# A two-layer decoder trunk on one core: eight heads' values in one wide projection, 64-row score matmuls for both heads of a pair, TensorE's attention order written out

## The chip, the core and the metric

The kernel runs on one core of a Trainium2 chip. A core has five engines with instruction streams of their own: TensorE (PE, matmuls; its weight loads are listed as PEld), VectorE (DVE), ScalarE (ACT), GpSimd (POOL) and SyncE (SP, which here issues the transfers). They meet through semaphores. Operands lie in SBUF, 128 partitions wide; matmul results go to PSUM, which has 8 banks of 128 x 512 fp32. The metric is the device time of one execution in microseconds, lower is better; three runs gave 951.81 to 952.43, median 952.17.

## The reference, cut to what matters

512 tokens of 1024 channels pass two layers, the first with a pooling mixer, the second with stick-breaking attention over 16 heads of 64, each followed by a squared-ReLU MLP of width 4096. Keys and values are projected once, from the stream behind the first MLP. The attention layer is where the change lies:

```python
kv = jnp.matmul(rms_norm(x, kv_norm_g), w_kv).reshape(B, S, 2, N_HEADS, HEAD_DIM)
...
q = jnp.matmul(h, w_q[j])
...
z = jnp.einsum('bhqd,bhkd->bhqk', q_blk, k_blk) * inv_sqrt_d        # 128 queries at a time
mask = s_idx < t_idx
log1m = jnp.where(mask, -jax.nn.softplus(z), 0.0)
excl = lax.cumsum(log1m, axis=3, reverse=True) - log1m
a = jnp.where(mask, jnp.exp(jax.nn.log_sigmoid(z) + excl), 0.0)
outs.append(jnp.einsum('bhqk,bhkd->bhqd', a, v_blk))
...
m = jnp.matmul(o, w_o[j])
```

## The kernel before

**Precision.** Every large product is made from operands split into a high part, rounded to the matmul format `F32R`, and the low remainder: high x high, high x low and low x high, three matmuls, added up in PSUM (`mm3`, lines 299 to 302; `up_block`, lines 703 to 717). ACT writes the high part (a copy), DVE the low one (a subtraction). The normed stream stands transposed in `xnh` and `xnl`: 128 channels on the partitions, 8 such chunks (`KC`), 512 tokens.

**Weights.** `want` (line 187) queues the blocks, 128 x 1024 each, in the order of use; `fill` (line 246) starts fetching the next while fewer than four (`ahead`) are held. There are three buffers with the tag `w` and one with `wx`, each for a high and a low part. Most blocks of the attention stage were scaled and split during the first MLP and put to DRAM (`kept`), so they come back as two transfers of 512 KB on SP's queue, and the transfer waits until the last matmul that read the buffer is done.

**The attention stage** goes by pairs of heads, 8 of them, in an order written as a list of steps (`ATT_ORDER`, line 59):

- `V`: values. One `V` group holds 4 heads, 256 columns, and two weight blocks (`values`, line 882). The digits behind the group are the tiles of 128 tokens; `V001` is group 0, tiles 0 and 1. Each tile takes 24 matmuls of 256 columns. ACT and DVE then write the two parts to a tile of tag `v`, of which there are two.
- `N2`, `N3`: the transposes of the normed token tiles 2 and 3, which the first MLP leaves undone.
- `K0`: the first half of the key projection of pair 0, for tokens 0 to 255 (`start`, line 904).
- `P`: keys, then queries of a pair (`queries_keys`, line 931), 24 matmuls of 512 columns each. For head a, ACT writes the high part of the keys twice, to both 64-partition halves of `k`, and DVE the low part to one half of `kl`, whose other half holds zeros. The queries' high part goes to one half of `q`, their low part to the other.
- `S`: scores, weights and scan (`weights`, line 1065). With the layout of `P`, one matmul over 128 rows gives high x high and low x high at once, and one against `kl` gives high x low. Per head these are 2 matmuls for each of 4 query tiles, of 512, 384, 256 and 256 columns, in three PSUM banks (`Head.scores`, line 985). Then ACT takes two sigmoids of them (`against`, `for_`), DVE scans (line 1016) and multiplies (line 1022).
- `T`: 20 transposes of a pair's weights by TensorE into six PSUM banks (line 1035), which ACT and DVE split into `ah` and `al` (lines 1041 and 1045).
- `A`: products with the values, 16 matmuls (line 1052).
- `O`: the output projection of two pairs; the digits are token tiles. `O00123` is that of pairs 0 and 1. `E1` is the end.

On TensorE the order is kept as written only up to `P0`; behind it, the scheduler that builds the program places TensorE's instructions itself by a model of their times, as it does for the other engines. So the order in the trace differs a little from the list: scores of pair 4 stand among products of pair 3, for instance. Within the end (`END_ORDER`, line 72, from the scores of the last pair on) all engines are ordered by hand; there `z01` is the scores of head 0, bank 1.

Of the kernel before, what the change touches and what calls it, by code (L numbers as in the profile page):

```python
# [15 lines left out]
P = 128  # L16
# [89 lines left out]
def trunk(ctx, tc, x, consts, grow, pw, wup, wdn, wq, wk, wv, wo, out):  # L106
# [12 lines left out]
    def name(s):  # L119
        uid[0] += 1  # L120
        return f"{s}{uid[0]}"
# [65 lines left out]
    def want(key, src, scaled=None):  # L187
        queue.append((key, src, scaled))
# [64 lines left out]
    def get(key):  # L253
        while key not in made:
            make()
        return made.pop(key)

    for l in range(2):
        if l == 1:
            n = len(queue)  # L260
            for what, i, part in ATT_ORDER:
                if what == "V" and 0 in part:
                    for h in range(2):
                        want(("v", i, h), wv[i, h], gains(C_KV * KC + 4 * h, 4))
                elif what == "P":
                    want(("k", i), wk[i], gains(C_KV * KC, KC))
                    want(("q", i), wq[i], gains(C_MIX_PRE1 * KC, KC))
                elif what == "O" or what == "E":
# [610 lines left out]
    with tc.tile_pool(name="att", bufs=1, reuse_waits="tile") as ap:  # L879
        att_pool[0] = ap  # L880

        def values(u, part):
            if u not in vs:
                w = [get(("v", u, h)) for h in range(2)]
                vs[u] = w, ap.tile([P, T, 4, 2, HD], F32R, tag="v", bufs=2, name=name("v"))
            w, v = vs[u]
            for s in part:
                need(s)
# [7 lines left out]
                pv4 = pv[:, :256].rearrange("p (h d) -> p h d", h=4)  # L896
                nc.scalar.copy(v[:, s, :, 0, :], pv4)
                nc.vector.tensor_tensor(
                    out=v[:, s, :, 1, :], in0=pv4, in1=v[:, s, :, 0, :].bitcast(F32), op=ALU.subtract
                )  # L900

        started = {}

        def start(key):

            need(0, 1)
            started[key] = ps(), get(key)
            up_block(*started[key], slice(0, S // 2))

        def project(key):  # L910
            need(*range(T))
            if key in started:
                pq, w = started.pop(key)
                up_block(pq, w, slice(S // 2, S))
            else:
                pq = ps()
                up_block(pq, get(key), slice(0, S))
            return pq

        def qk_tile(tag):  # L920
# [2 lines left out]
        half = [slice(0, HD), slice(HD, P)]  # L923


        kls = [qk_tile(f"kl{a}") for a in range(2)]
        with tc.issue_after(latest["pool"].ins):
            for a in range(2):
                nc.gpsimd.memset(kls[a][half[1 - a], :].bitcast(F32), 0.0)

        def queries_keys(p):
            qs, ks = [], []
            pk = project(("k", p))
            for a in range(2):
                k, kl, own, other = qk_tile(f"k{a}"), kls[a], half[a], half[1 - a]
                nc.scalar.copy(k[own, :], pk[own, :])
                latest["act"] = nc.scalar.copy(k[other, :], pk[own, :])
                latest["dve"] = nc.vector.tensor_tensor(
                    out=kl[own, :], in0=pk[own, :], in1=k[own, :].bitcast(F32), op=ALU.subtract
                )  # L940
                ks.append(k)
            fill()
            pq = project(("q", p))
            for a in range(2):
                q, own, other = qk_tile(f"q{a}"), half[a], half[1 - a]
                latest["act"] = nc.scalar.copy(q[own, :], pq[own, :])
                latest["dve"] = nc.vector.tensor_tensor(
                    out=q[other, :], in0=pq[own, :], in1=q[own, :].bitcast(F32), op=ALU.subtract
                )
                qs.append(q)  # L950
            fill()
            return qs, ks
# [19 lines left out]
        class Head:  # L972
# [12 lines left out]
            def scores(self, b):  # L985
                q, k, kl = self.qk[0][self.a], self.qk[1][self.a], kls[self.a]
                pz = self.pz[b] = ps()
                o = 0
                for i in self.SCORES[b][0]:
                    n = max(256, (i + 1) * P)  # L990
                    nc.tensor.matmul(pz[:, o : o + n], q[:, TS[i]], k[:, :n], start=True, stop=False)  # L991
                    nc.tensor.matmul(pz[:, o : o + n], q[:, TS[i]], kl[:, :n], start=False, stop=True)  # L992
                    o += n

            def against(self, b):
                tiles, at = self.SCORES[b]
# [64 lines left out]
            def out(self, o):  # L1061
                own = half[self.a]
                nc.vector.tensor_tensor(out=o[own, :], in0=self.po[half[0], :], in1=o[own, :], op=ALU.add)

        def weights(p):
# [43 lines left out]
        def end():  # L1109
# [82 lines left out]
            def half_up(j):  # L1192
# [2 lines left out]

            last_heads = heads[last]
            steps = {
                "z": lambda a, b: last_heads[a].scores(b), "x": lambda a, b: last_heads[a].against(b),
                "y": lambda a, b: last_heads[a].for_(b), "sc": lambda a: last_heads[a].scan(),
                "mu": lambda a: last_heads[a].weigh(), "T": lambda a, b: last_heads[a].turn(b),  # L1200
                "ah": lambda a, b: last_heads[a].high(b), "al": lambda a, b: last_heads[a].low(b),
# [25 lines left out]

        def step(what, i, part):
            nonlocal gpost1
            if what == "V":  # L1230
                values(i, part)
            elif what == "N":
                need(i)
            elif what == "K":
                start(("k", i))
            elif what == "P":
                qk[i] = queries_keys(i)
                if i == PAIRS - 1:
                    until(("o", 5))
            elif what == "S":  # L1240
                gate[0] = True
                heads[i] = weights(i)
                fill()
            elif what == "T":
                transposed(heads[i])
                behind.update(latest)
            elif what == "A":
                mix_pair(i, vs[i // 2][1])
            elif what == "O" and part:
                out_proj(i, part)  # L1250
                if i == 0:
# [68 lines left out]
```

## Time and profile before

| | us |
|---|---|
| time, median of 3 runs | 952.17 |
| lowest and highest of them | 951.81, 952.43 |
| the profiled execution, its own time | 952.24 |
| its span, first to last instruction | 950.5 |

The page's groups of the operations that the change touches (line, engine, operation, out<-in and shape, count | busy us in total, mean ns of one | idle us before them):

```profile
L300 PE MATMUL ps<-w,xnh 128*128 128x256 f32 x128 | 36.6, 286 | 0.0
L991 PE MATMUL ps<-k,q 128*128 128x256 f32 x32 | 8.4, 284 | 0.0
L991 PE MATMUL ps<-k,q 128*128 128x512 f32 x16 | 6.5, 409 | 0.0
L938 DVE TENSOR_TENSOR kl<-ps,k 64x512 fp32r<-64x512 f32 x16 | 11.0, 685 | 15.1 <-ACT k L937 15.0
L947 DVE TENSOR_TENSOR q<-ps,q 64x512 fp32r<-64x512 f32 x16 | 11.0, 688 | 7.5 <-ACT q L946 7.2
L1016 DVE TENSOR_TENSOR_SCAN e<-u,begin 128x1280 f32<-128x1280 f32 x16 | 45.2, 2823 | 11.0 <-ACT u L1000 10.4
```

Times are microseconds from the start of the span. A matmul record lasts longer than its share of TensorE, since the next one starts before it ends; what a matmul costs in a stream is read from start to start. The attention stage runs from about 368 to 570 us, the last pair's end to about 640, between the two MLPs.

### The profile page before, as it was taken

The numbers are of one execution on the slowest core, as the hardware profiler recorded it, in microseconds if no ns is written. First come the engines' busy times: TensorE is split into PE (matmuls) and PEld (weight loads), VectorE is DVE, ScalarE is ACT, GpSimd is POOL, SyncE is SP. The second block draws the span as 40 slices with busy tenths as digits, with TensorE's granted clock in tenths as the row PEclk, the third lists the DMA queues.
The fourth block names the chain that finished last, engine by engine and source line by source line (L and its number), as shares of the span: only waits on it lengthen the run. The fifth ranks groups of instructions, "written<-read, shape, count | busy, mean of one in ns | idle before, by whom it ended". The sixth has DMA issues, their size and how long they took to land.

```text
span 950.5 us, 12510 instructions
## 1 busy us (share of the span) xinstructions
PE 940.9 (99%) x4758; PEld 799.7 (84%) x4758; DVE 707.9 (74%) x813; ACT 577.8 (61%) x1015; POOL 42.1 (4%) x85
## 2 busy tenths in 40 slices
PE   9999999999999999999999999999999999999996
PEld 7998888888888889899899988898888888888885
DVE  5875798988979976476577778874696966958756
ACT  6667979788775547456656554865545444444532
POOL 2300000000000004000000000200000000000002
PEclk9999999999999999999999999999999999999999
DMA  8244969789697760522424271442513233133102
GB/s 309 96 178 148 342 219 347 295 283 356 217 323 269 271 207 2 202 85 90 172 95 178 91 264 45 134 155 71 196 43 131 93 133 111 45 133 111 35 11 89
DMA packets 43262, 156.15 MB, mean 164 GB/s; under 512 B 4289, under 2 KB 4673, under 8 KB 43202
## 3 DMA queue, kind: packets, MB, share of 16 engines
q1 hardware_dynamic: 43202, 155.36, 46.1%
q8 instruction: 37, 0.61, 0.3%
q14 instruction: 23, 0.19, 0.1%
HBM read 121.79 MB, written 33.55 MB: 163 GB/s over the span
## 4 chain that ended last, share of the span: by engine, by line
PE 94%; DVE 2%; ACT 2%; POOL 1%; issue 1%; POOLq 0%; DVEq 0%; ACTq 0%
PE ps L589 28%; PE ps L708 15%; PE ps L712 15%; PE ps L711 15%; PE ps L300 4%; PE ps L301 4%; PE ps L302 4%; PE ps L1052 2%; PE ps L829 1%; PE ps L1035 1%; PE ps L991 1%; PE ps L395 1%; PE ps L992 1%; ACT xn L285 1%; PE ps L801 1%
## 5 line engine op out<-in xcount | busy, mean ns | idle before, releaser
L589 PE MATMUL ps<-w,a 128*128 128x512 f32 x1176 | 278.6, 389 | 0.0
L711 PE MATMUL ps<-xnh,w 128*128 128x512 f32 (+1 forms) x712 | 261.1, 369 | 0.0
L712 PE MATMUL ps<-xnl,w 128*128 128x512 f32 (+1 forms) x712 | 261.1, 368 | 0.0
L708 PE MATMUL ps<-xnh,w 128*128 128x512 f32 (+1 forms) x712 | 260.3, 368 | 0.1
L589 PEld LDWEIGHTS ps<-w,a 128*128 128x128 f32 x1176 | 220.7, 188 | 45.9 <-DVE w L282 0.2
L712 PEld LDWEIGHTS ps<-xnl,w 128*128 128x128 f32 x712 | 134.2, 189 | 21.8
L708 PEld LDWEIGHTS ps<-xnh,w 128*128 128x128 f32 x712 | 133.7, 189 | 22.4 <-DVE w L850 0.3
L711 PEld LDWEIGHTS ps<-xnh,w 128*128 128x128 f32 x712 | 133.8, 189 | 22.1
L598 DVE TENSOR_TENSOR y<-ps,y 128x512 f32<-128x512 f32 x124 | 84.5, 688 | 43.9 <-PE ps L589 43.7
L172 DVE TENSOR_TENSOR w<-raw,w 128x1024 fp32r<-128x1024 f32 x58 | 70.9, 1223 | 57.4 <-ACT w L170 57.2
L170 ACT CAST w<-raw 128x1024 fp32r<-128x1024 f32 x58 | 61.0, 1051 | 79.3 <-PE ps L708 79.2
L281 ACT CAST a<-r 128x768 fp32r<-128x768 f32 (+1 forms) x60 | 47.7, 794 | 72.1 <-PE ps L589 55.7
L282 DVE TENSOR_TENSOR a<-r,a 128x768 fp32r<-128x768 f32 (+1 forms) x60 | 54.1, 902 | 12.3 <-ACT a L281 12.1
L281 ACT CAST w<-e 128x1536 fp32r<-128x1536 f32 (+1 forms) x30 | 41.8, 1394 | 23.8 <-DVE e L563 14.4
L1016 DVE TENSOR_TENSOR_SCAN e<-u,begin 128x1280 f32<-128x1280 f32 x16 | 45.2, 2823 | 11.0 <-ACT u L1000 10.4
L282 DVE TENSOR_TENSOR w<-e,w 128x1536 fp32r<-128x1536 f32 (+1 forms) x30 | 49.5, 1649 | 1.8 <-ACT w L281 1.6
L181 ACT ACTIVATE apart<-apart,eye 128x128 f32<-128x128 f32 (+1 forms) x132 | 43.1, 407 | 0.5 <-DMA apart<-in_wk 0.5
L282 DVE TENSOR_TENSOR w<-w,w 128x1536 fp32r<-128x1536 f32 (+1 forms) x20 | 33.0, 1650 | 8.6 <-ACT w L281 8.6
L621 ACT ACTIVATE r<-ps 128x512 f32<-128x512 f32 x56 | 33.1, 591 | 8.6 <-PE ps L708 8.5
L282 DVE TENSOR_TENSOR w<-xn,w 128x1536 fp32r<-128x1536 f32 (+1 forms) x20 | 33.0, 1650 | 5.6 <-ACT w L281 5.5
L300 PE MATMUL ps<-w,xnh 128*128 128x256 f32 x128 | 36.6, 286 | 0.0
L622 ACT ACTIVATE r<-r 128x512 f32<-128x512 f32 x56 | 35.5, 634 | 1.3
(134 smaller groups left out, 1393.6 us busy)
## 6 DMA issues: line engine op xcount, KB each, us to landing
raw<-in_wup SPq DMA_DIRECT2D x64, 512.0 KB, 4.1
w<-kept SPq DMA_DIRECT2D x60, 512.0 KB, 4.2
kept<-wx SPq DMA_DIRECT2D x30, 512.0 KB, 5.0
w<-in_wdn SPq DMA_DIRECT2D x8, 1536.0 KB, 6.7
kept<-apart SPq DMA_DIRECT2D x24, 512.0 KB, 5.7
xn<-in_wdn SPq DMA_DIRECT2D x8, 1536.0 KB, 7.7
apart<-in_wk SPq DMA_DIRECT2D x7, 512.0 KB, 7.1
apart<-in_wq SPq DMA_DIRECT2D x7, 512.0 KB, 9.4
```

The costliest lines, as they stand in the source:

```text
L170: nc.scalar.copy(hi, raw)
L172: nc.vector.tensor_tensor(out=lo, in0=raw, in1=hi.bitcast(F32), op=ALU.subtract)
L181: nc.scalar.mul(c, c, gc[:, lo + k : lo + k + 1])
L281: latest["act"] = nc.scalar.copy(hi, src)
L282: latest["dve"] = nc.vector.tensor_tensor(out=lo, in0=src, in1=hi.bitcast(F32), op=ALU.subtract)
L300: nc.tensor.matmul(dst, ah, bh, start=start, stop=False)
L589: nc.tensor.matmul(bank, a[:, x, q, TS[t]], w[:, z, q], start=start and q == 0 and k == 0, stop=q == self.n - 1 and k == 2, skip_group_che ...
L598: nc.vector.tensor_tensor(out=part, in0=bank, in1=part, op=ALU.add)
L708: nc.tensor.matmul(pu[:, cols], wl[:, k, :], xnh[:, k, cols], start=False, stop=k == KC - 1)
L711: nc.tensor.matmul(pu[:, cols], wh[:, k, :], xnh[:, k, cols], start=k == 0, stop=False)
L712: nc.tensor.matmul(pu[:, cols], wh[:, k, :], xnl[:, k, cols], start=False, stop=False)
L1016: nc.vector.tensor_tensor_scan(out=self.e[:, ::-1], data0=self.u[:, 1:][:, ::-1], data1=begin[:, ::-1], initial=0.0, op0=ALU.mult, op1=ALU ...
```

## The change

1. The values of the first 8 heads are projected together, 512 columns at a time, as step `H`: `H0` adds up chunks 0 to 3, `H1` chunks 4 to 7, the digits behind are token tiles. A tile is 12 matmuls of 512 columns per step. The four weight blocks of this half are laid out anew on the host, two chunks of 512 columns in each, and are all held until the half is done; `H` ends with a `fill` of four blocks. It stands ahead of the first projections and scores. Steps `K0` and its `start` go. The other 8 heads keep `V`.
2. `queries_keys` writes high and low parts of both heads as whole 128-partition tiles (`kh`, `kl`, `qh`, `ql`): one copy on ACT and one subtraction on DVE for the keys, and as many for the queries. `scores` makes three 64-row matmuls per head and query tile, the two heads in turn, each on its own half of the partitions and into its own bank, with 512, 384, 256 and 128 columns. All scores of a pair are made before any sigmoid is issued; the order of sigmoids, scans and multiplications is altered with that.
3. TensorE's order is kept as written for the whole list, which itself is altered: `S` follows `P0` at once, `S` and `A` follow `T` at `T0`, `T1` and `T3`, and `O0` is split around `T2`. In the end the scores of both heads are one step (`z1` for `z01` and `z11`).

```diff
-    for w in """V001 N2 K0 N3 V02 P0 V03 S0 P1 T0 V101 S1 A0 P2 T1 V123 A1 S2 P3 T2 O00123 A2 S3 P4 V201 T3 A3
-    S4 P5 T4 V223 S5 A4 P6 V301 T5 S6 A5 V323 P7 T6 E1""".split()
+    for w in """H001 N2 H101 N3 H023 H123 P0 S0 P1 T0 S1 A0 P2 T1 S2 A1 P3 O001 T2 O023 S3 A2 P4 V201 T3 S4
+    A3 P5 V22 T4 V23 S5 A4 P6 V30 T5 V31 S6 A5 V323 P7 T6 E1""".split()
...
-    for w in """D6 R0 R1 z01 z00 x01 z02 x00 z11 x02 z12 y02 sc0 A60 y01 y00 x11 z10 oc60 A61 y11 x10 od60 E01 y10
+    for w in """D6 R0 R1 z1 z0 x01 z2 x00 x02 y02 sc0 A60 y01 y00 x11 oc60 A61 y11 x10 od60 E01 y10
...
+                if what == "H" and not i and 0 in part:
+                    for h in range(4):
+                        want(("v", 0, h), wv[h], gains(C_KV * KC + 2 * h, 2))
...
+        def half_values(i, part):
+            if not half_w:
+                half_w.extend(get(("v", 0, h)) for h in range(4))
+                for u in range(2):
+                    vs[u] = None, value_tile(u)
+            for s in part:
+                if i == 0:
+                    half_bank[s] = ps()
+                for k in range(4 * i, 4 * i + 4):
+                    (wh, wl), c = half_w[k // 2], NS[k % 2]
+                    mm3(
+                        half_bank[s], xnh[:, k, TS[s]], xnl[:, k, TS[s]], wh[:, c], wl[:, c], k == 0, k == KC - 1
+                    )
+                if i == 1:
+                    for u in range(2):
+                        value_parts(vs[u][1], s, half_bank[s][:, u * 256 : u * 256 + 256])
+            if i == 1 and T - 1 in part:
+                fill(ahead)
...
         def queries_keys(p):
+            both = []
+            for what in "kq":
+                src = project((what, p))
+                hi, lo = qk_tile(f"{what}h"), qk_tile(f"{what}l")
+                latest["act"] = nc.scalar.copy(hi, src)
+                latest["dve"] = nc.vector.tensor_tensor(out=lo, in0=src, in1=hi.bitcast(F32), op=ALU.subtract)
+                both.append((hi, lo))
+                fill()
+            return both
...
+        def scores(hs, b):
+            (kh, kl), (qh, ql) = hs[0].qk
+            for x in hs:
+                x.pz[b] = ps()
+            o = 0
+            for i in Head.SCORES[b][0]:
+                n = SEG[i][1]
+                for m, (x, y) in enumerate(((qh, kh), (qh, kl), (ql, kh))):
+                    for h in hs:
+                        own = half[h.a]
+                        nc.tensor.matmul(
+                            h.pz[b][:, o : o + n], x[own, TS[i]], y[own, :n], start=m == 0, stop=m == 2,
+                        )
+                o += n
...
         def weights(p):
             hs = [Head(qk[p], p, a) for a in range(2)]
+            for b in range(3):
+                scores(hs, b)
             for x in hs:
                 for b in range(3):
-                    x.scores(b)
                     x.against(b)
+            hs[0].scan()
+            for x in hs:
+                for b in range(3):
                     x.for_(b)
-                x.scan()
-                x.weigh()
+            hs[0].weigh()
+            hs[1].scan()
+            hs[1].weigh()
             return hs
...
-        first = [what for what, _, _ in ATT_ORDER].index("P") + 1
         with tc.manual_schedule(engines={mybir.EngineType.PE}):
-            for x in ATT_ORDER[:first]:
+            for x in ATT_ORDER[:-1]:
                 step(*x)
-        for x in ATT_ORDER[first:-1]:
-            step(*x)
         end()
```

More of the change, by code (lines that the diff above doesn't have):

```diff
@@ L261, in trunk @@
             for what, i, part in ATT_ORDER:
-                if what == "V" and 0 in part:
+                if what == "H" and not i and 0 in part:
+                    for h in range(4):
+                        want(("v", 0, h), wv[h], gains(C_KV * KC + 2 * h, 2))
+                elif what == "V" and 0 in part:
                     for h in range(2):
-                        want(("v", i, h), wv[i, h], gains(C_KV * KC + 4 * h, 4))
+                        want(("v", i, h), wv[2 * i + h], gains(C_KV * KC + 4 * h, 4))
                 elif what == "P":
@@ L267, in trunk @@
                     want(("q", i), wq[i], gains(C_MIX_PRE1 * KC, KC))
-                elif what == "O" or what == "E":
+                elif what == "O" and 0 in part or what == "E":
                     for c in range(2 * i, 2 * i + 2 if what == "O" else PAIRS):
@@ L880, in trunk, with value_tile, value_parts @@
         att_pool[0] = ap
+        def value_tile(u):
+            return ap.tile([P, T, 4, 2, HD], F32R, tag="v", bufs=2, name=name("v"))
+        def value_parts(v, s, src):
+            pv4 = src.rearrange("p (h d) -> p h d", h=4)
+            nc.scalar.copy(v[:, s, :, 0, :], pv4)
+            nc.vector.tensor_tensor(
+                out=v[:, s, :, 1, :], in0=pv4, in1=v[:, s, :, 0, :].bitcast(F32), op=ALU.subtract
+            )
+        half_w, half_bank = [], {}
+        def half_values(i, part):
[16 more added lines that the diff above has]
+                fill(ahead)
         def values(u, part):
             if u not in vs:
-                w = [get(("v", u, h)) for h in range(2)]
-                vs[u] = w, ap.tile([P, T, 4, 2, HD], F32R, tag="v", bufs=2, name=name("v"))
+                vs[u] = [get(("v", u, h)) for h in range(2)], value_tile(u)
             w, v = vs[u]
             for s in part:
-                need(s)
                 pv = ps()
@@ L895, in values @@
                     )
[L896 to L908, printed above, removed]
-        def project(key):
[L911 to L917, printed above, removed]
+                value_parts(v, s, pv[:, :256])
+        def project(key):
+            pq = ps()
+            up_block(pq, get(key), slice(0, S))
             return pq
@@ L923, in trunk @@
         half = [slice(0, HD), slice(HD, P)]
[L926 to L929, printed above, removed]
         def queries_keys(p):
[L932 to L952, printed above, removed]
+            both = []
[7 more added lines that the diff above has]
+            return both
         begin = ap.tile([P, NSEG], mybir.dt.bfloat16, tag="begin", name="begin")
@@ L983, in __init__ @@
                 self.pz, self.pt, self.parts, self.to = {}, {}, {}, {}
[L985 to L993, printed above, removed]
             def against(self, b):
@@ L1197, in end @@
             steps = {
-                "z": lambda a, b: last_heads[a].scores(b), "x": lambda a, b: last_heads[a].against(b),
+                "z": lambda b: scores(last_heads, b), "x": lambda a, b: last_heads[a].against(b),
                 "y": lambda a, b: last_heads[a].for_(b), "sc": lambda a: last_heads[a].scan(),
@@ L1229, in step @@
             nonlocal gpost1
-            if what == "V":
+            if what == "H":
+                half_values(i, part)
+            elif what == "V":
                 values(i, part)
@@ L1233, in step @@
                 need(i)
-            elif what == "K":
-                start(("k", i))
             elif what == "P":
@@ L1250, in step @@
                 out_proj(i, part)
-                if i == 0:
+                if gpost1 is None:
                     with tc.issue_after(latest["sp"].ins):
                         gpost1 = gain_row(R_MIX_POST1)
-        first = [what for what, _, _ in ATT_ORDER].index("P") + 1
         with tc.manual_schedule(engines={mybir.EngineType.PE}):
-            for x in ATT_ORDER[:first]:
+            for x in ATT_ORDER[:-1]:
                 step(*x)
-        for x in ATT_ORDER[first:-1]:
-            step(*x)
         end()
@@ L1289 @@
     blocks = lambda w, n: w.reshape(KC, P, -1, n).transpose(2, 1, 0, 3)
-    wv = blocks(a["w_kv"][:, D:], 256).reshape(4, P, 2, D).transpose(0, 2, 1, 3)
+    wv = np.concatenate([
+        blocks(w, n).reshape(-1, P, c, D).transpose(0, 2, 1, 3).reshape(4, P, D)
+        for w, n, c in ((a["w_kv"][:, D : D + 512], 512, 4), (a["w_kv"][:, D + 512 :], 256, 2))
+    ])
     arrays = {
```

1 line of the change is left out of this document (added).

## Prediction

> **What bounds the kernel now.** I read the page first: how busy each engine is, the granted clock, and the chain that ended last by engine.
>
> ```profile
> span 950.5 us, 12510 instructions
> PE 940.9 (99%) x4758; PEld 799.7 (84%) x4758; DVE 707.9 (74%) x813; ACT 577.8 (61%) x1015; POOL 42.1 (4%) x85
> PEclk9999999999999999999999999999999999999999
> PE 94%; DVE 2%; ACT 2%; POOL 1%; issue 1%; POOLq 0%; DVEq 0%; ACTq 0%
> ```
>
> TensorE is busy 99% of the span at full clock and holds 94% of the chain. DVE and ACT have room. So an edit pays if it shortens TensorE's own stream, and costs if it opens a hole in it. The second view is busy time by window, cut at the steps of the attention stage (a count includes a record or two that reach in from a neighbour):
>
> ```profile
> core 0: us, PE busy (x) PEld busy (x) DVE busy (x) ACT busy (x) POOL busy (x), PEclk, DMA share, GB/s
> 392.91:395.47 2.56, 2.56 (x18) 2.38 (x17) 0.42 (x1) 2.27 (x6) 0.00 (x0) 1.00 0.90 266
> 395.47:406.37 10.90, 10.90 (x50) 8.97 (x49) 9.23 (x5) 5.33 (x14) 0.00 (x0) 1.00 0.71 269
> 406.37:408.47 2.10, 2.10 (x21) 2.10 (x20) 1.65 (x3) 2.08 (x5) 0.00 (x0) 1.00 0.43 92
> 414.30:416.87 2.57, 2.57 (x19) 2.39 (x18) 0.42 (x1) 2.21 (x6) 0.00 (x0) 1.00 0.00 0
> 416.87:419.38 2.51, 2.51 (x19) 2.33 (x17) 2.02 (x1) 2.51 (x9) 0.00 (x0) 1.00 0.00 0
> 456.41:468.00 11.59, 11.55 (x51) 8.98 (x49) 4.82 (x9) 6.72 (x14) 0.00 (x0) 1.00 0.19 73
> ```
>
> In order: the 16 score matmuls of pair 0; the 48 projection matmuls of pair 1; the 20 transposes of pair 0; the scores of pair 1; the products of pair 0; the first output projection. In all but the last TensorE has no hole. The waits of the stage hold little that can be won back:
>
> ```profile
> PEld ps L300 <- DVE al L1045: 0.5, 1, 0.5
> PE ps L991 <- DVE q L947: 0.4, 1, 0.4
> ```
>
> **Part 1: the value projection.** A 24-matmul block of 256 columns against projections of 512 columns:
>
> ```profile
> 368.46:371.34 2.88, 2.88 (x26) 1.00 0.00 0
> ```
>
> A narrow matmul costs 2.88/24 = 0.120 us, a wide one 10.90/48 = 0.2271. Eight heads need 192 narrow ones now (4 tiles x 24 x 2 groups) = 23.04 us, and 96 wide ones after = 21.80: -1.24 us. Dropping step K0 makes key block 0 one wide block instead of two narrow halves: 48 x 0.120 - 5.45 = -0.31 us. The transposes of tiles 2 and 3 stay, each behind a 24-matmul block of 5.45 us, where the first has 5.75 now: no hole. The same 8 + 8 small evacuations of these values remain on ACT and DVE, in windows where both are half idle: nothing.
>
> The weights: the four blocks of the half take all four weight buffers, so key block 0 can only be fetched when the first is free, after 18 of the 24 matmuls of step H023; H123 (5.45 us) and the rest of H023 (1.36 us) cover it, 6.8 us.
>
> ```profile
> w<-kept SPq DMA_DIRECT2D x60, 512.0 KB, 4.2
> ```
>
> A block is two such transfers, 4.2 us each and partly side by side. Covered, so 0; uncovered it would be some 5 us, once. The next blocks queue behind it on SP in order of use, one every 5.45 us. From there on the number of blocks held ahead is what it was: 0.
>
> **Part 2: the score matmuls.** Per pair now 2.57 us. What each width costs:
>
> ```profile
> 415.82 0.39 PE L992 MATMUL ps<-kl,q 128*128 128x512 f32 x1
> 416.05 0.33 PE L991 MATMUL ps<-k,q 128*128 128x384 f32 x1
> 416.22 0.34 PE L992 MATMUL ps<-kl,q 128*128 128x384 f32 x1
> 416.39 0.28 PE L991 MATMUL ps<-k,q 128*128 128x256 f32 x1
> 416.51 0.28 PE L992 MATMUL ps<-kl,q 128*128 128x256 f32 x1
> ...
> 417.93 0.23 PE L1052 MATMUL ps<-ah,v 128*128 128x128 f32 x1
> 417.99 0.27 PE L1052 MATMUL ps<-al,v 128*128 128x128 f32 x1
> 418.10 0.45 PE L1052 MATMUL ps<-ah,v 128*128 128x512 f32 x1
> ```
>
> From start to start: 512 columns 0.23, 384 0.17, 256 0.12, 128 0.06 where its weights were there and 0.11 where the next had to come. The weight loads set that last number:
>
> ```profile
> 417.93 0.19 PEld L1052 LDWEIGHTS ps<-al,v 128*128 128x128 f32 x1
> 418.04 0.19 PEld L1052 LDWEIGHTS ps<-ah,v 128*128 128x128 f32 x1
> 418.15 0.19 PEld L1052 LDWEIGHTS ps<-al,v 128*128 128x128 f32 x1
> ```
>
> Loads do not start closer than 0.11 us. The change needs 12 couples of 64-row matmuls per pair (three products, four query tiles), the 256 columns of tile 0 cut to 128. No row shows 64-row matmuls, so bounds. Lower: the two heads of a couple run side by side on their own rows and banks, loads too: 3 x (0.227 + 0.172 + 0.12 + 0.11) = 1.89 us per pair. Upper: each matmul costs what a 128-row one costs: 3.77. Between: matmuls side by side, loads one after another, 0.22 per couple: 3 x (0.227 + 3 x 0.22) = 2.66. I take the lower end. The nearest row is the 128-row matmul itself, which streams through all rows what a couple streams through the two halves, and the rows show a load running beside a matmul. 8 x (1.89 - 2.57) = -5.4 us. The middle gives +0.7, the upper +9.6.
>
> The Trainium skill, "TensorE: Matmul & The Clock Gate", Part 3 on packing small matmuls, says that matmuls on different row groups run concurrently, starting within about 4 ns, and gives 3.07 times for four 32-row matmuls. By it the sum would stand at the lower end; no trace here shows it.
>
> Entering and leaving the 64-row shape is new too: 16 changes (eight score steps). The nearest row is the change from transposes to ordinary matmuls:
>
> ```profile
> 375.00 0.36 PE L711 MATMUL ps<-xnh,w 128*128 128x256 f32 x1
> 375.20 0.28 PE L712 MATMUL ps<-xnl,w 128*128 128x256 f32 x1
> ```
>
> The first takes 0.20 instead of 0.12: 0.08. I take 16 x 0.08 = +1.3 us. Lower bound 0. Upper: the array runs empty (0.39 of a wide record less its step of 0.227 = 0.16) and the next load is exposed (0.19): 0.35 x 16 = 5.6.
>
> The evacuations of queries and keys fall from six 64-partition copies on ACT and four subtractions on DVE per pair to two and two. They lie beside the busy TensorE, so they bring 0, except where a fixed order waits for them.
>
> **Part 3: TensorE's order written out.** Two new neighbours matter. P0 is followed at once by S0; now value tile V03 stands between. How long after a projection its queries are ready is seen at pair 7:
>
> ```profile
> 561.40 0.39 PE L708 MATMUL ps<-xnh,w 128*128 128x512 f32 x1
> 561.63 2.35 PE L1035 MATMUL ps<-eye,w 128*128 128x128 f32 x20
> 561.89 0.58 ACT L946 CAST q<-ps 64x512 fp32r<-64x512 f32 x1 [2.34 <-PE ps L708]
> 562.50 0.69 DVE L947 TENSOR_TENSOR q<-ps,q 64x512 fp32r<-64x512 f32 x1 [2.23 <-ACT q L946]
> ```
>
> TensorE was free at 561.63, the high part was there at 562.47, the low part at 563.19. With S0 directly behind: 0.9 us until the first two products start, these take 0.45, then 0.2 for the low part: +1.1 us. All scores of the stage queue behind it.
>
> Second, T0, T1 and T3 are followed at once by the next pair's scores and then products. There are 8 PSUM banks; the transposes hold 6, the scores want 6. The banks come free with DVE's low parts:
>
> ```profile
> 408.20 1.62 DVE L1045 TENSOR_TENSOR al<-ps,ah 128x512 fp32r<-128x512 f32 x3
> 410.57 1.62 DVE L1045 TENSOR_TENSOR al<-ps,ah 128x512 fp32r<-128x512 f32 x3
> ```
>
> Three cost 1.62 us, the last is done 5.8 us after the transposes began (406.37), with four pieces of keys and queries in between. With one query piece (0.7) ahead of them, I put the six at 2.05, 2.7, 3.1, 3.7, 4.3 and 4.7 us. Scores take the two free banks at 2.1, two more at 2.75, the last two at 3.7 and end at 4.4; the products end at 6.9 where 2.10 + 1.89 + 2.51 = 6.5 is the bare sum: 0.4 us x 3 = +1.2. The last pair's scores behind T6 have a wait like it now (0.4): unchanged. Bounds 0 and, if the scores wait for the last bank, 3.7 each.
>
> In exchange the output projection, 11.59 us for 48 matmuls (10.90 without a wait), is split around T2, whose own chain then gets 5.45 us more: -0.6. T0 keeps its cover. The second weighing ends at 404.91, 1.5 us ahead of T0; with scores shorter by 0.7 and a chain no earlier, 0.8 is left, and the head that it serves is turned 1 us into T0:
>
> ```profile
> 403.42 1.49 DVE L1022 TENSOR_TENSOR w<-w,e 128x1280 f32<-128x1280 f32 x1
> ```
>
> **Sum**, against the profiled execution (952.24, its span 950.5 and 1.7 around it; the median is 952.17): -1.24 - 0.31 - 5.4 + 1.3 + 1.1 + 1.2 - 0.6 = -3.95, so 948.3 us.
>
> **Rivals.**
>
> *Each change of shape empties TensorE.* 5.6 in place of 1.3: +0.35, 952.6 us. For it: every matmul here has one shape and the record tail of 0.16 us is hidden only by the next matmul of that shape. Against it: transposes and matmuls change places for 0.08. The Trainium skill, "TensorEngine Tiling (Array Packing)", Key Properties, says that changing the tiling mode drains TensorE; the trace cannot agree or disagree.
>
> *Matmuls side by side, loads in a row.* +0.7 in place of -5.4, and the bank waits vanish in the longer scores (-1.2): +0.95, 953.2 us. For it: loads 0.11 apart without exception. Against it: those all use the whole height of the array.
>
> *No concurrency: the change does not do what it says.* +9.6, no bank waits: -1.24 - 0.31 + 9.6 + 1.3 + 1.1 - 0.6 = +9.85, 962.1 us. For it: one matmul starts after another in every row. Against it: disjoint rows, operands and banks.
>
> *The fixed order turns PSUM into the bound.* At T0, T1 and T3 the scores wait until the last low part is out, 5.8 - 2.1 = 3.7 us each, 11.1 in place of 1.2: +5.95, 958.2 us. It decides from 1.7 us per place. For it: in the trace TensorE slips other work in between. Against it: half of the pieces that stood ahead of the low parts are gone.
>
> **How the numbers follow.** Forecast 0.50, emptying 0.12, loads 0.14, no concurrency 0.12, PSUM 0.12. No change is what lies within 0.2% (1.9 us, about what a measurement of this kernel can tell): 950.3 to 954.1. Faster: 0.49 of the forecast and 0.01 of the emptying, 0.50. Same: 0.01 of the forecast, 0.10 of the emptying, half of the loads (0.07), 0.02 of PSUM, 0.20. Slower: the rest, 0.30. The forecast's own range is 944 (no change cost, no new wait) to 952.6. The whole range runs to 957, where loads in a row meet most of the emptying or PSUM waits of 3.3 us each; outside are the no-concurrency case and part of PSUM, about 0.2.
>
> **What would show it.** A score step of about 2 us, its matmul records in couples starting together; 4 us would mean no concurrency, 2.7 loads in a row. A hole of 0.1 against 0.35 us on each side of the score steps. A wait of TensorE for ACT or DVE behind P0 of about 1 us. Waits of scores for L1045's low parts behind T0, T1 and T3, 0.4 or 3.7 us. Wide value matmuls 0.227 apart. A wait of P0 for a transfer would prove my cover wrong.

## The result and the profile after

The changed kernel takes 955.20 us (median of 8 runs, 954.05 to 955.54) beside 951.97 for the kernel before (8 runs, 951.63 to 952.43): a ratio of 1.0032, 95% interval 1.0022 to 1.0042. It is 3.2 us slower. That lies in the range forecast, with the wrong sign. The profiled execution took 955.53 us, its span is 953.8. Six of the eight runs took 955.03 to 955.54 at a mean granted clock of 0.995 or 0.996, the profiled one among them, and two 954.05 and 954.13 at 0.999 and 0.997.

The page after: span; busy time by engine; the largest group of matmuls, which had no idle time before the change and has 2.4 us now (idle us stand last).

```profile
span 953.8 us, 12326 instructions
PE 939.6 (99%) x4702; PEld 790.7 (83%) x4702; DVE 695.8 (73%) x797; ACT 557.1 (58%) x975; POOL 41.1 (4%) x83
L592 PE MATMUL ps<-w,a 128*128 128x512 f32 x1176 | 279.2, 389 | 2.4 <-ACT a L284 2.4
```

TensorE does 1.3 us less and the span is 3.3 us longer: holes. The only large one is not in the attention stage. L592, before the change L589, is the second product of an MLP, the squares (`a`) times the down weights (`w`). So I cut the span in stages by TensorE's first matmuls. Timeline of TensorE, before, at the first of these products in the second MLP (the value projection's start, 368.46, stands in the prediction's windows):

```profile
641.02 0.39 PE L589 MATMUL ps<-w,a 128*128 128x512 f32 x1
```

The same places after, the first value matmul and that product:

```profile
372.62 0.39 PE L303 MATMUL ps<-w,xnh 128*128 128x512 f32 x1
...
644.35 0.62 PE L592 MATMUL ps<-w,a 128*128 128x512 f32 x2
```

The value projection starts 4.16 us late, and from there to the second MLP it takes 271.73 us in place of 272.56. The whole loss arises in the first MLP, whose own products the change does not touch, and the attention stage gains only 0.83 of the 3.95 forecast.

**The first MLP.** ACT's timeline of the stretch, before (start, duration, line, tile; in brackets its idle time and who ended it):

```profile
179.18 0.84 ACT L281 CAST a<-r 128x768 fp32r<-128x768 f32 x1 [1.97 <-DVE r L544]
181.54 1.06 ACT L170 CAST w<-raw 128x1024 fp32r<-128x1024 f32 x1 [1.52 <-PE ps L708]
```

ACT after:

```profile
181.78 1.04 ACT L170 CAST w<-raw 128x1024 fp32r<-128x1024 f32 x1 [4.33 <-PE ps L711]
...
183.22 0.82 ACT L284 CAST a<-r 128x768 fp32r<-128x768 f32 x1
```

TensorE after:

```profile
181.35 0.39 PE L711 MATMUL ps<-xnh,w 128*128 128x512 f32 x1
184.09 1.32 PE L592 MATMUL ps<-w,a 128*128 128x512 f32 x4 [2.35 <-ACT a L284]
```

Before, ACT writes the high part of `a`, which the next product multiplies, and then splits a weight block (L170), whose buffer TensorE has first to leave. After, the two have changed places: ACT sits 4.33 us in front of L170, and `a` is ready 4 us later. TensorE stands for 2.35 us. ACT's order is not the whole of it: `r`, which `a` is made from, comes 2.25 us later from DVE. DVE's timeline, before and after:

```profile
178.19 0.95 DVE L544 TENSOR_TENSOR r<-r 128x768 f32<-128x768 f32 x1
```

```profile
180.44 0.95 DVE L547 TENSOR_TENSOR r<-r 128x768 f32<-128x768 f32 x1
```

Windows of the ten us from 180, after, and of a part of them (columns as in the prediction):

```profile
180.00:185.00 5.00, 2.65 (x12) 1.90 (x11) 5.00 (x6) 3.22 (x5) 0.00 (x0) 1.00 0.59 210
185.00:190.00 5.00, 5.00 (x17) 3.92 (x16) 5.00 (x6) 4.96 (x11) 0.00 (x0) 0.66 0.52 103
185.01:188.42 3.41, 3.41 (x10) 2.63 (x9) 3.41 (x4) 3.41 (x8) 0.00 (x0) 0.50 0.36 24
```

Behind the hole the granted clock is 0.66 in the mean of five us, 0.50 for 3.41 of them, and 17 matmul records stand where the kernel before has 24 in its windows; 7 x 0.227 = 1.6 us more. 2.35 + 1.6 make 3.95 of the 4.16.

**The attention stage.** Windows after, in order: P0; S0; T0; S2, behind T1; S3. (By the same view S1, behind T0, took 2.26, and the two halves of O0 5.60 and 5.78.)

```profile
396.17:407.89 11.72, 11.04 (x50) 8.83 (x48) 1.56 (x4) 1.92 (x4) 0.00 (x0) 1.00 0.76 287
407.89:410.22 2.33, 2.33 (x24) 1.78 (x25) 0.67 (x1) 1.07 (x3) 0.00 (x0) 1.00 0.86 304
421.22:423.91 2.69, 2.47 (x21) 2.09 (x19) 2.69 (x4) 2.39 (x6) 0.00 (x0) 1.00 0.54 166
442.02:445.90 3.88, 3.01 (x25) 1.93 (x24) 3.88 (x7) 3.88 (x11) 0.00 (x0) 1.00 0.02 4
472.96:475.03 2.07, 2.07 (x26) 1.87 (x25) 0.00 (x0) 1.61 (x4) 0.00 (x0) 1.00 0.75 253
```

S3 has nothing to wait for: 24 matmuls in 2.07 us. Its start and end on TensorE's timeline, with the neighbours:

```profile
472.63 0.40 PE L305 MATMUL ps<-w,ohl 128*128 128x512 f32 x1
472.96 0.50 PE L1065 MATMUL ps<-kh,qh 64*128 64x512 f32 x2
473.29 0.39 PE L1065 MATMUL ps<-kl,qh 64*128 64x512 f32 x2
...
474.71 0.27 PE L1065 MATMUL ps<-kl,qh 64*128 64x128 f32 x2
474.82 0.28 PE L1065 MATMUL ps<-kh,ql 64*128 64x128 f32 x2
475.03 0.50 PE L1040 MATMUL ps<-ah,v 128*128 128x512 f32 x1
```

A couple (x2) of 128 columns takes 0.11, and the twelve 1.89 without the changes of shape: what as many 128-row matmuls take by the steps in the prediction. At a change of shape the step before and the step behind are each 0.10 longer: 472.63 to 472.96 and 472.96 to 473.29 are 0.33 in place of 0.23; 474.82 to 475.03 is 0.21 in place of 0.11, and the first product takes 0.33, to 475.36. That is 0.2 us a change.

S2 is the step that waits. DVE's timeline around it:

```profile
440.07 1.22 DVE L172 TENSOR_TENSOR w<-raw,w 128x1024 fp32r<-128x1024 f32 x1
...
441.80 1.22 DVE L172 TENSOR_TENSOR w<-raw,w 128x1024 fp32r<-128x1024 f32 x1
442.93 3.14 DVE L1033 TENSOR_TENSOR al<-ps,ah 128x512 fp32r<-128x512 f32 x6
```

The low parts that free the PSUM banks (L1033) stand behind two low parts of weight blocks (L172): output blocks 0 and 1, the two that are not split ahead.

### The profile page after: what moved, and what is told of

It reads as the page before. It is cut to its first block, busy times and chain, and to the rows that moved or that the text cites. A ratio compares the mean times of both kernels' runs of the same rounds, so it can differ in the third digit from the quotient of the medians.

```text
span 953.8 us, 12326 instructions
## 1 busy us (share of the span) xinstructions
PE 939.6 (99%) x4702; PEld 790.7 (83%) x4702; DVE 695.8 (73%) x797; ACT 557.1 (58%) x975; POOL 41.1 (4%) x83
## 4 chain that ended last, share of the span: by engine, by line
PE 92%; DVE 3%; ACT 2%; POOL 1%; DMA 1%; issue 1%; SPq 0%; POOLq 0%; DVEq 0%; ACTq 0%
PE ps L592 28%; PE ps L714 15%; PE ps L711 15%; PE ps L715 14%; PE ps L303 4%; PE ps L305 4%; PE ps L304 4%; PE ps L1040 2%; PE ps L1065 2%; PE ps L1023 2%; PE ps L832 1%; PE ps L398 1%; ACT xn L288 1%; DMA band<-in_consts 1%; PE ps L804 1%
## 5 line engine op out<-in xcount | busy, mean ns | idle before, releaser
L592 PE MATMUL ps<-w,a 128*128 128x512 f32 x1176 | 279.2, 389 | 2.4 <-ACT a L284 2.4
L592 PEld LDWEIGHTS ps<-w,a 128*128 128x128 f32 x1176 | 220.7, 188 | 48.5 <-ACT a L284 2.8
L172 DVE TENSOR_TENSOR w<-raw,w 128x1024 fp32r<-128x1024 f32 x58 | 70.8, 1221 | 58.9 <-ACT w L170 58.8
L170 ACT CAST w<-raw 128x1024 fp32r<-128x1024 f32 x58 | 61.0, 1051 | 85.2 <-PE ps L711 85.1
L284 ACT CAST w<-e 128x1536 fp32r<-128x1536 f32 (+1 forms) x30 | 41.9, 1396 | 23.7 <-DVE e L566 14.3
L181 ACT ACTIVATE apart<-apart,eye 128x128 f32<-128x128 f32 (+2 forms) x122 | 41.3, 420 | 0.0
L288 ACT ACTIVATE xn<-y 128x512 f32<-128x512 f32 (+1 forms) x25 | 15.3, 613 | 32.2 <-DVE y L470 28.6
```

The costliest lines, as they stand in the source:

```text
L170: nc.scalar.copy(hi, raw)
L172: nc.vector.tensor_tensor(out=lo, in0=raw, in1=hi.bitcast(F32), op=ALU.subtract)
L284: latest["act"] = nc.scalar.copy(hi, src)
L592: nc.tensor.matmul(bank, a[:, x, q, TS[t]], w[:, z, q], start=start and q == 0 and k == 0, stop=q == self.n - 1 and k == 2, skip_group_che ...
```

## The experiments

The theory: the reordered list of weight blocks costs the first MLP some 4 us, and the attention stage as changed is worth 1 us or less, because changes of shape cost 0.2 and S2 waits. The rival: the attention stage itself is worse, and the hole is an accident of the profiled execution.

**a_both: the changed kernel with the old splitting order.** The list `apart` had the four value blocks of the half first; here the four projection blocks of pairs 0 and 1 go back between the first two and the last two, and the value blocks are scaled in four pieces as before.

```diff
...
-                        want(("v", 0, h), wv[h], gains(C_KV * KC + 2 * h, 2))
+                        want(("v", 0, h), wv[h], gains(C_KV * KC + 2 * h, 2, 2))
...
             apart.extend(x for x in queue[n:] if x[0] not in [("o", c) for c in range(2)])
+            apart[2:8] = apart[4:8] + apart[2:4]
```

> The changed kernel with the blocks that the first MLP splits ahead put back into the old order (the second two value blocks behind the keys and queries of pair 1) and each value block scaled in four pieces of 256 columns again instead of two of 512. Attention is untouched. Theory (the loss of 4.2 us lies in the first MLP, where ACT's order changed with that list): the hole at 181 us goes, the attention stage starts at 368.5 us as before the change, and the time falls by 4.2 us to 951.0. Rival (the hole is a chance of one execution, the loss lies in the attention stage): 955.2, as the changed kernel.

Measured: 951.55 us (950.93 to 954.01, 11 runs), ratio 0.9998 [0.9989, 1.0007]: 3.65 us below the changed kernel. The hole is gone, by the window of this kernel:

```profile
180.00:185.00 5.00, 5.00 (x23) 4.13 (x22) 5.00 (x6) 3.44 (x5) 0.00 (x0) 1.00 0.61 210
```

**b_order: the kernel before with nothing but the new order.**

```diff
             apart.extend(x for x in queue[n:] if x[0] not in [("o", c) for c in range(2)])
+            apart[2:8] = apart[6:8] + apart[2:6]
```

> The kernel before, with nothing altered but the order in which the first MLP splits blocks ahead: values of group 1 now before keys and queries of pair 0. The same instructions in number and shape. Theory (the order of that list alone decides ACT's order in the first MLP): a hole near 181 us, TensorE at half clock behind it, 952.0 + 4.2 = 956.2 us. Rival (it takes the wider scaling pieces or the changed attention stage): 952.0.

Measured: 954.94 us (954.57 to 956.1, 5 runs), ratio 1.0034 [1.0021, 1.0046]. The same hole comes in a kernel whose attention stage is untouched. Windows of it:

```profile
180.00:185.00 5.00, 2.65 (x12) 1.90 (x11) 5.00 (x7) 3.28 (x5) 0.00 (x0) 1.00 0.61 212
185.00:190.00 5.00, 5.00 (x23) 4.13 (x23) 5.00 (x6) 4.91 (x11) 0.00 (x0) 1.00 0.52 136
```

Taken away, together with the wider scaling pieces, the order gives 3.65 us back; put in alone, it makes 2.9 us and the hole. That settles the place of the loss and that the order alone is enough for it; the scaling pieces alone were not run. The hole came here without a reduced clock (1.00), so the two are not one thing.

**a_defer: a_both, with the two output blocks split behind S2.**

```diff
                 both.append((hi, lo))
-                fill()
+                if p != 2:
+                    fill()
...
                 heads[i] = weights(i)
-                fill()
+                fill(3 if i == 2 else 1)
```

> The first kernel of this call (old splitting order), with the fetch and split of the first two output-projection blocks moved from the projections of pair 2 to behind the scores of pair 2. Theory (the two splits on ACT and DVE stand ahead of the low parts that free PSUM banks, 2.45 us on DVE, and hold the scores of pair 2 back by 1.8 us): that score step falls from 3.9 to about 2.1 us and the time by 1.6 to 949.4. Rival (banks come free no sooner, or the output projection waits for its blocks instead): 951.0 or more.

Measured: 949.62 us (949.4 to 950.38, 10 runs), ratio 0.9976 [0.9966, 0.9985], 1.9 below a_both. S2 took 2.30, by its window:

```profile
438.53:440.83 2.30, 2.30 (x26) 1.97 (x25) 2.30 (x6) 2.30 (x5) 0.00 (x0) 1.00 0.02 7
```

So the banks of S2 were late because of the splits queued ahead, not because eight are too few for it. S1 has no split ahead of it and takes 2.92 here, as in a_both, 0.85 more than 2.07; what would shorten it was not tried.

**a_samehalf: a_both, both heads' score matmuls on the first half of the rows.** Head 1's scores are then made of head 0's queries and keys.

```diff
-                        own = half[h.a]
+                        own = half[0]
```

> The changed kernel with the old splitting order (951.55), both heads' score matmuls reading the same half of the partitions, so that the second head of each pair gets the first head's scores. Same shapes and number. Theory (a 64-row matmul overlaps another only on the other half, whatever the order of issue): all 24 of a step run one after another, 3.77 instead of 1.89 us, +1.9 x 8 = +15, 966.6 us. Rival (what brings the couples together is the order or the weight loads, not the halves): 951.5.

Measured: 965.89 us (one run), 14.3 above a_both. Its step S3 takes 3.98 us, of TensorE's timeline:

```profile
474.15 0.72 PE L1067 MATMUL ps<-kh,qh 64*128 64x512 f32 x2
474.71 0.62 PE L1067 MATMUL ps<-kl,qh 64*128 64x512 f32 x2
475.18 0.62 PE L1067 MATMUL ps<-kh,ql 64*128 64x512 f32 x2
...
478.13 0.50 PE L1042 MATMUL ps<-ah,v 128*128 128x512 f32 x1
```

From couple to couple it is 0.47 at 512 columns, on different rows 0.23 (468.59 to 468.82 in the next experiment). Concurrency is worth 1.91 us a pair here, loads included. (Of the 14.3, some 1.6 are a slowed clock: it is 0.50 from 445.65 to 449.06, and a_both's profile has no such stretch. Eight pairs would be 15.3; the longer steps take some of the waits away, as S1 shows, which takes 3.98 too.)

**a_inturn: a_both, with the heads one after the other.** For each query tile the three products of head 0 are issued, then those of head 1.

```diff
-                for m, (x, y) in enumerate(((qh, kh), (qh, kl), (ql, kh))):
-                    for h in hs:
+                for h in hs:
+                    for m, (x, y) in enumerate(((qh, kh), (qh, kl), (ql, kh))):
```

> The first kernel of this call, with the three 64-row products of one head issued before those of the other, instead of in turn. Same matmuls. Theory (two 64-row matmuls run side by side only when neighbours in the stream use different halves): only the neighbours at the change of head overlap; serial 3.77 us per pair less 0.63 within and 0.40 between query tiles is 2.74 against 1.89, +0.85 x 8 = +6.8 us, 957.8. If nothing overlaps any more: 3.77, +15, 966. Rival (order of issue does not matter, the array takes any free half): 951.0.

Measured: 950.68 us (one run), the rival's time. TensorE's timeline of S3:

```profile
468.26 0.50 PE L1067 MATMUL ps<-kh,qh 64*128 64x512 f32 x2
468.59 0.40 PE L1067 MATMUL ps<-kl,qh 64*128 64x512 f32 x2
468.82 0.40 PE L1067 MATMUL ps<-kh,ql 64*128 64x512 f32 x2
...
470.33 0.50 PE L1042 MATMUL ps<-ah,v 128*128 128x512 f32 x1
```

The records show the same couples, and the step takes the same 2.07: the matmul issued fourth starts with the first. Where a matmul has to wait, the order does count. At S0 the first two of head 0 start when the queries' high part is there, and the third waits for the low part. Head 1's first, issued fourth, could have started with the first; it starts with the third, at 403.63, and S0 takes 2.80 us for 2.31 in a_both:

```profile
402.90 0.50 PE L1067 MATMUL ps<-kh,qh 64*128 64x512 f32 x1 [0.68 <-ACT qh L950]
...
403.63 0.66 PE L1067 MATMUL ps<-kh,qh 64*128 64x512 f32 x2
```

**a_free: a_both, TensorE's order left to the scheduler behind P0.**

```diff
-            for x in ATT_ORDER[:-1]:
+            for x in ATT_ORDER[: ATT_ORDER.index(("P", 0, [])) + 1]:
                 step(*x)
+        for x in ATT_ORDER[ATT_ORDER.index(("P", 0, [])) + 1 : -1]:
+            step(*x)
```

> The changed kernel with the old splitting order (951.55), TensorE's order kept as written only up to the first projections and placed by the scheduler behind them, as before the change. Undoes part 3 alone. Theory (the written order costs the waits behind T0, T1 and the scores of pair 2, about 3 us): these waits are filled with other matmuls, 949 us, unless the interleaving brings more changes between 64-row and full matmuls at 0.2 us each. Rival (the order costs nothing, the waits are PSUM's and come back): 951.5 or more.

Measured: 955.88 us (954.68 to 957.17, 5 runs), ratio 1.0043 [1.0031, 1.0056], 4.3 above a_both. The scheduler puts the products with `ql` of S0 between projections of pair 1, and T0 then waits. Of TensorE's timeline:

```profile
406.83 0.79 PE L1067 MATMUL ps<-kh,ql 64*128 64x512 f32 x6
...
420.93 1.30 PE L1025 MATMUL ps<-eye,w 128*128 128x128 f32 x10 [3.10 <-DVE w L1012]
```

The granted clock is 0.50 from 422.07 to 425.48, behind this wait, and again from 445.96 to 449.37, so the loss of the profiled execution is in part waits and in part a slowed clock.

**b_scores: the kernel before with part 2 alone**, the new queries, keys and scores, TensorE's order by the scheduler as it was.

```diff
         def weights(p):
             hs = [Head(qk[p], p, a) for a in range(2)]
+            for b in range(3):
+                scores(hs, b)
             for x in hs:
                 for b in range(3):
-                    x.scores(b)
                     x.against(b)
...
```

> The kernel before with part 2 alone: whole-height keys and queries and 64-row score matmuls of both heads in turn; values, step order and scheduling as before. Theory (a step of 2.07 us and 0.2 lost around it for 2.57, -0.3 x 8 = -2.4, and no new waits since tiles of values stand between): 949.6 us. Rival 1 (scoring side by side at no cost of change, -5.4): 946.6. Rival 2 (six banks at once cost what is won): 952.

Measured: 958.18 us (956.31 to 958.34, 5 runs), ratio 1.0055 [1.0042, 1.0069]. The scheduler mixes the scores of pair 4 with products of pair 3, as it did before, and tears the couples apart; TensorE's timeline:

```profile
497.08 0.39 PE L1047 MATMUL ps<-kh,ql 64*128 64x512 f32 x1
497.40 0.44 PE L1022 MATMUL ps<-al,v 128*128 128x384 f32 x1
...
497.89 0.49 PE L1047 MATMUL ps<-kh,qh 64*128 64x512 f32 x1
```

Head 0 runs at 497.08, head 1 at 497.89, each alone (x1) with a change of shape on either side. Windows of the same work, scores of pair 4 and products of pair 3, in the kernel before and in this one:

```profile
491.84:497.03 5.19, 5.19 (x36) 4.84 (x34) 3.33 (x7) 4.62 (x12) 0.00 (x0) 1.00 0.00 0
```

```profile
495.47:503.83 8.36, 8.36 (x43) 5.68 (x42) 3.15 (x7) 6.21 (x13) 0.00 (x0) 1.00 0.00 0
```

3.2 us go here. 2.6 more go to a wait of T2 for the weighing, by its line of TensorE's waits (total, times, longest):

```profile
PE ps L1005 <- DVE w L992: 3.4, 2, 2.6
```

From 457.67 to 461.08, in that wait and behind it, the granted clock is 0.50, so T2 takes 5.88 us in place of 2.10.

**b_fixed: b_scores with the changed order of ACT's and DVE's steps and TensorE's order written out, but narrow values, which stand in the gaps**, and the list of blocks ahead as before.

```diff
+    for w in """V001 N2 K0 N3 V02 P0 V03 S0 P1 T0 V101 S1 A0 P2 T1 V123 S2 A1 P3 O001 T2 O023 S3 A2 P4 V201 T3
+    S4 A3 P5 V22 T4 V23 S5 A4 P6 V30 T5 V31 S6 A5 V323 P7 T6 E1""".split()
...
```

> The kernel before with parts 2 and 3 but not part 1: 64-row scores, TensorE's order as written, with narrow value tiles left between P0 and S0, T0 and S1, T1 and S2, and the output projection split around T2. Theory (what 64-row scores lose without a written order is the couples torn apart and the late scans; with the order written and tiles of values in the gaps, the waits of 1.06, 0.85 and most of 1.82 us go and part 1's 1.5 us are given up): 951.55 - 3.7 + 1.5 = 949.4. Rival (64-row scores lose whatever the order, since each change of shape costs): 952 or more.

Measured: 950.35 us (949.93 to 951.67, 11 runs), ratio 0.9982 [0.9973, 0.9991]. Without the wide values, and with tiles of narrow ones ahead of S0, S1 and S2, it is faster than the kernel before. The list, TensorE's order and that of ACT and DVE differ from b_scores at once, so the run does not say which of them turned the loss. Its largest wait in this stage is again for the split of an output block, 0.8 us, now at the output projection.

**a_h13: a_both, with the last value tile between P0 and S0**, and **a_defer_h13**, with a_defer's edit as well.

```diff
-    for w in """H001 N2 H101 N3 H023 H123 P0 S0 P1 T0 S1 A0 P2 T1 S2 A1 P3 O001 T2 O023 S3 A2 P4 V201 T3 S4
+    for w in """H001 N2 H101 N3 H023 H12 P0 H13 S0 P1 T0 S1 A0 P2 T1 S2 A1 P3 O001 T2 O023 S3 A2 P4 V201 T3 S4
```

> The changed kernel with the old splitting order (951.55), the last tile of the wide value projection (2.7 us) moved between the projections and the scores of pair 0. Theory A: the wait of 1.06 us for the first queries is covered, 950.5. Theory B: two weight buffers come free only then, so the keys' block of pair 1 lands some 5 us after its buffer is free and its projection, due 3.4 us after, waits 1 to 2.5 us: 951.5 to 953.

> The two changes of order that shortened a wait each (output blocks split behind the scores of pair 2; last wide value tile between projections and scores of pair 0), on the changed kernel with the old splitting order. Theory (the two waits are in different places and add up): 949.6 - 0.6 = 949.0. Rival (the later start of pair 1's block eats it): 949.6 or more.

Measured: a_h13 950.93 us (950.51 to 952.64, 10 runs), ratio 0.9992 [0.9983, 1.0001]; a_defer_h13 949.52 us (948.8 to 949.99, 7 runs), ratio 0.9972 [0.996, 0.9983]. a_h13 lies 0.6 below a_both, less than the runs of either scatter. Its S0 no longer waits (2.05 us, from 403.58), but part of the gain goes to transfers, since the value blocks' buffers come free a tile later. A line of TensorE's waits:

```profile
PE ps L713 <- DMA w<-kept: 0.7, 2, 0.4
```

On top of a_defer it gives 0.1, less than the runs scatter. The two versions with a_defer's edit are the fastest of all that ran, 2.4 to 2.6 us below the kernel before.

## Why the prediction was wrong

**The step that failed** is the zero for the weight blocks: "The next blocks queue behind it on SP in order of use, one every 5.45 us. From there on the number of blocks held ahead is what it was: 0." It followed the list in the attention stage, where it is fetched, and there it held: P0 shows no wait for a transfer. The same list sets in which order the blocks are scaled and split during the first MLP (`split_apart`), on ACT and DVE. That stage was never costed. a_both and b_order put it at 3.65 and 2.9 us, the profile at 4.16, of which 1.6 is a slowed clock that the profile of b_order does not show. Without it the changed kernel stands where the kernel before does. The forecast missed by 6.9 us; this is a little over half of it, and the other 3.1 us are what the attention stage fell short of its 3.95.

Why the new order makes the scheduler swap `a` and L170 stays open. The blocks differ in their scaling (eight pieces for keys and queries, fewer for values), so ACT's load in each slot moves; but that this tips its model was not tried.

**Right in kind, mis-sized:**
- Changes of shape: 0.08 each, 1.3 in all. Measured 0.2, 3.2 us in all; the rival with emptying had 0.35. The transposes, on whose row the 0.08 rested, have 128 rows like their neighbours; they were the wrong nearest row. Where transposes stand ahead, the step before is longer by more: T1 takes 2.27 for 2.10.
- Bank waits, 0.4 at each of three places. Measured against 2.07: S1 0.2, S2 1.8, S4 0.1 (2.14 in its window), 2.1 in place of 1.2. S2 alone passed the 1.7 from which the PSUM rival was to decide, and a_defer, in which S2 takes 2.30, shows that the splits ahead of L1033 made most of it.
- T0's cover: said to hold, cost 0.6 (2.69 for 2.10; 0.4 beside the 2.27 of T1). The prediction took DVE's chain to be no earlier; it came later. ACT now takes the sigmoids of both heads in turn, and the first scan of pair 0 starts at 413.29, 3.1 us behind S0's end, where it was 0.5 (395.97, 395.47).
- The split output projection: -0.6 forecast; 5.60 + 5.78 = 11.38 against 11.59, -0.2.

**Right:**
- Couples of 64-row matmuls run side by side, loads too: 1.89 us a pair without the changes of shape, and a_samehalf prices the lack of it at 14.3 us, 1.6 of it slowed clock, against the 13.8 between the forecast and that rival. Loads in a row fall with the same rows: a couple of 128 columns takes 0.11, the spacing of one load and not of two. (That the loads before are "0.11 apart without exception" said too much: four loads of transposes, from 595.57 on, take 0.42 together.)
- S0 behind P0: 11.72 - 10.90 + 2.33 - 2.07 = 1.08 for 1.1.
- Wide values: in the changed kernel the stretch from 372.62 to 396.17 holds 96 matmuls and two sets of transposes of 0.79, so 21.97 us for 21.80 forecast.

With these sizes, and step K0's -0.31 as forecast, the terms of the attention stage add up to -1.07 - 0.31 - 5.4 + 3.2 + 1.08 + 2.1 + 0.6 - 0.2 = 0.0, where the stage shows -0.83. Most of the 0.8 between lies in the score steps. Summed up on TensorE's timeline, all eight took 21.6 us in the kernel before, 1.0 more than 8 x 2.57, chiefly at the last pair, whose matmuls took 2.86 + 0.51 with a wait of 0.41. The same step takes 2.31 in the changed kernel, 0.24 over 2.07, which the terms leave out as well. One bound of the prediction is summed up wrongly: without cost of change and new waits its own terms give 944.7, not 944. The order written out, which the prediction counted only as a source of waits, is what the gain depends on: a_free and b_scores lose 4 to 6 us without it, the slowed clock behind their waits included.

## What to carry to other kernels

A list that says in which order data is used may also order work in an earlier stage: find every reader of it before its reordering is costed at nothing. Side-by-side 64-row matmuls pay at full rate if they stay together, at 0.2 us for each change of shape; a scheduler that tears the couples apart, as in b_scores, gives the gain back and more, so the order is best written out. Once it is, look at what stands on the other engines ahead of the piece that frees a buffer: moving two weight splits brought 1.9 us.

## What the runs showed of the hardware

Each half of the rows works off its own matmuls: in a_inturn a matmul of the upper half started with one issued three places before it, and the step took 2.07 us as in the other order. At S0, where the third matmul of the lower half had to wait for its operand, the first of the upper half, issued behind it, started with it, 0.73 us after the step's first. The Trainium skill, "TensorE: Matmul & The Clock Gate", Part 3, says that matmuls start and end strictly in program order; for two halves of the rows these records disagree, as far as modelled ends allow, and the step's length, which does not hang on them, does too.

A change between 64 and 128 rows costs 0.10 us on either side of it where wide matmuls are the neighbours (S3). "TensorEngine Tiling (Array Packing)" of the Trainium skill, Key Properties, says that a change of mode drains TensorE; the trace agrees that a change costs time, 0.2 us, but does not tell a drain from weight loads that no longer run ahead.

Ahead of the last microseconds of a kernel, the granted clock fell to 0.50 in four of the profiles, each time for 3.41 us: from 185.01 in the changed kernel, behind a hole of 2.35 us; from 457.67 in b_scores, within a hole of 2.61; from 422.07 in a_free, behind a hole of 3.10, and from 445.96 there, where TensorE was idle for only 0.46 of the five us before; and from 445.65 in a_samehalf, where it was idle for 0.16. In b_order a hole of 2.35 us in the same place was followed by 1.00. What decides between them no run here shows.
